# Short products of constants in TensorE's idle time, placed by the scheduler

## The chip, the cores and the metric

The kernel runs on one core of a Trainium2 chip. The metric is the device time of one execution in microseconds (us), as the median of several runs. A core has five engines that work side by side and wait for one another through semaphores: TensorE (PE) for matrix products, VectorE (DVE), ScalarE (ACT), GpSimd (POOL), and SyncE (SP), which issues the DMA transfers. PE reads its operands from SBUF and writes its results to PSUM, a memory of eight banks of 128 partitions by 512 columns of float32.

## What is computed

Two transformer blocks in a row, each with two layers, on 512 tokens of width 1024, in float32. Cut to the shape of the work:

```python
def first_block(x, ...):
    h = x
    for l in range(2):
        u = rms_norm(h, attn_norm[l])
        proj = u @ w_in[l]                       # 1024 -> 7424 columns
        a = differential_attention(...)          # 4 heads
        r = bidirectional_retention(...)         # 4 heads
        c = grouped_query_attention(...)         # 8 query heads, 2 key heads
        merged = sum(sigmoid(gate_n) * (branch_n @ w_branch[l, n]) for n, branch_n in enumerate((a, r, c)))
        h = h + merged @ w_out[l]
        m = relu(rms_norm(h, mlp_norm[l]) @ w_mlp_in[l]) ** 2
        h = h + m @ w_mlp_out[l]
    return h

def second_block(x, c, ctx, ...):                # ctx: 256 more tokens, updated in the first layer only
    for l in range(2):
        z = modulate(rms_norm(x, norm1_g[l]), ...) @ w_in[l]
        y_f, y_a, y_c = fourier_mix(...), latent_attention(...), conformer_conv(...)
        x = x + gate1 * (concat(y_f, y_a, y_c) @ w_o[l])
        x = x + gate2 * (relu(modulate(rms_norm(x, norm2_g[l]), ...) @ w_mlp1[l]) ** 2 @ w_mlp2[l])
    return rms_norm(x, final_norm_g)
```

## The kernel before

Activations lie transposed: 128 features on the partitions, tokens along the free dimension, so that 1024 features are eight tiles. Every product is done in three passes of float32r operands: a value is split into a high part (an ACT copy, `hi`) and a rest (a DVE subtraction, `lo`), and high by high, high by rest and rest by high are added up in PSUM. A weight tile of 128x1024 comes by DMA into one of three `raw` buffers, ACT writes its high part and DVE its rest into a pair of six `w` buffers (`wload`), and PE multiplies. The three passes of one step are a group: its first two products need the weight's high part, the third needs the rest that DVE writes.

The work is cut into phases: the mixer of a layer (`m10`, `m11` in the first block, `m20`, `m21` in the second) and its output projection with the MLP (`p10`, `p11`, `p20`, `p21`). Each phase has PSUM pools of its own, whose tags (`mm`, `sc`, `acc` and others) share the eight banks. Between phases the next norm is worked out in two halves of 256 tokens (`norm_split`, `factor`): squares of the features are split into a pair `x`, PE adds them over the features by a product with constants (`sums`; printed as `x,sums`), DVE takes the root in some ten short steps, and the scaled values become the operands `r` of the next phase. The last pair `x` of the second half is thus the head of a chain of PE, DVE and ACT steps that the next phase waits for.

No engine's order is written by hand. The code records its operations into a planner (`Sched`), and `run` plays a phase through on a time line of its own: each operation has a cost (`_cost`), each engine takes the ready operation of least priority number, a buffer is given when it is free on that time line. The order in which operations start there is the order in which the instructions are emitted; on the chip each engine then works through its own list in order, and waits where an operand isn't there. The time line's costs are estimates, so that an engine's idle time on it need not be idle time on the chip. A bank counts as free 0.2 us after the last step that reads it.

The constants `sums` (128x896: averages over 64, 128, 256 or 1024 features and centring matrices) come by DMA into a `raw` buffer and are copied by DVE (`V.tensor_copy(sums, ones)`, the CAST at 14.13 us in the trace).

Of the kernel before, what the change touches and what calls it, by code (L numbers as in the profile page):

```python
# [19 lines left out]
P = 128  # L20
# [36 lines left out]
HI = "A"  # L57
LO = "V"
YADD = "V"
HALVES = 'P'  # L60
SWAP8 = list(range(8, 16)) + list(range(8)) + list(range(16, 32))
SWAP16 = list(range(16, 32)) + list(range(16))
# [87 lines left out]
class Sched:  # L150


    def __init__(self, tc):
        self.tc, self.nc = tc, tc.nc
        self.tags, self.ops, self.bufs, self.bias, self.macro = {}, [], [], 0.0, None
        self.behind, self.dma, self.port = {}, 0.0, 0.0
        nc = tc.nc
        self.engines = {"PE": nc.tensor, "DVE": nc.vector, "ACT": nc.scalar, "POOL": nc.gpsimd, "SP": nc.sync}

# [111 lines left out]
    def run(self):  # L271
# [90 lines left out]
        def hold(op):  # L362
# [7 lines left out]
            coming[op.eng] = keep  # L370
            return until

        left = len(ops)
        while left:
            for e in self.engines:
                if free_at[e] > now:
                    continue
                while ready[e]:
                    op = ops[ready[e][0][1]]
                    until = None if e == "SP" else hold(op)  # L380
                    if until is not None:
                        heapq.heappush(events, (until, 0, 0))
                        break
                    heapq.heappop(ready[e])
                    if place(op):
                        order.append(op)
                        if e == "SP":
                            dma = max(dma, now + DMA) + op.cost
                            free_at[e], end = now + 0.06, dma
                        else:  # L390
                            end = free_at[e] = (max(now, port) if op.port else now) + op.cost
                            if op.port:
                                port = end
                        for n in op.nexts:
                            n.unstarted -= 1
                            n.soon = max(n.soon, end + lag(op, n))
                            if not n.unstarted:
                                coming[n.eng].append(n)
                        heapq.heappush(events, (free_at[e], 0, 0))
                        heapq.heappush(events, (end, 1, op.idx))  # L400
                        break
            if not events:
                raise RuntimeError(f"no step can go on: {left} left")
            now = events[0][0]
# [44 lines left out]
        base = free_at["PE"]  # L449
        self.behind, self.dma = {e: max(0.0, t - base) for e, t in free_at.items()}, max(0.0, dma - base)  # L450
        self.port = max(0.0, port - base)
        for b in {id(b): b for b in self.bufs}.values():
            b.at = max(0.0, b.at - base)
        for b in self.bufs:
# [68 lines left out]
def kernel(  # L523
# [42 lines left out]
    def fixed(p, cols, name, dt=F32):  # L566
        return sc.fixed(p.tile([P, cols], dt, tag=name, name=name))
# [119 lines left out]


    sums = fixed(gp, 7 * P, "sums", F32R)
    ones = sc.alloc("raw", 7 * P)  # L690
    SP.dma_start(ones, const_d[:, P:])
    V.tensor_copy(sums, ones)
# [992 lines left out]
    def phase(name, shares, slots=()):  # L1685

        with ExitStack() as st:
            p = pool(name, None, st)
            pp = pool(name + "p", bass.MemoryType.PSUM, st)
            banks.clear()  # L1690
            for tags, n in shares.items():
                tag = tags.split()[0]
                banks.update((x, tag) for x in tags.split())
                if tag == "sc2":
                    sc.slots(pp, tag, n, 1024, F32)
                    banks["sc"] = "sc2"
                else:
                    sc.slots(pp, tag, n, 512, F32)
# [267 lines left out]
```

## Time and profile before

| | us |
|---|---|
| median of 3 runs | 3541.93 |
| lowest, highest | 3540.41, 3547.73 |
| the profiled execution | 3539.29 |
| its span, first to last instruction | 3537.5 |
| PE busy in it | 3348.9 (95%) |
| DVE, ACT, POOL busy | 2285.2 (65%), 1437.3 (41%), 948.2 (27%) |
| mean granted clock of TensorE | 0.977 of full speed |

The profile is one execution, taken by the hardware's profiler. Times in it count from the span's start. A product's duration in it holds a modelled drain, so that the distance of two starts is the better measure of what a product takes in a row of products. In brackets behind a timeline row stands the idle time of the engine before it and who ended it; rows of one kind are merged, with their count behind an x. [...] All helper calls of the planner have one line number, so that groups are told apart by the tiles that they write and read (`mm<-r,w`: into a bank of tag mm, from operand r and weight w).

### The profile page before, as it was taken

Reading aid. Unit: us, or ns where it says so; the run is one execution under the profiler, and the core shown is the slowest. Engines: PE = TensorE matmul, PEld = TensorE weight load, DVE = VectorE, ACT = ScalarE, POOL = GpSimd, SP = SyncE. Lnnn points to the kernel's source line nnn. Section 1 sums busy time; section 2 is a strip of 40 time slices with the busy share of each in tenths; the row PEclk is TensorE's granted clock in tenths of the full one; section 3 lists DMA queues with packets and bytes.
Section 4 is the critical chain, followed back from the end, with each engine's and each line's share of the span. In section 5 each row is a group of like instructions: output and inputs, shape, how many; then the busy total and the mean of one; then the engine's idle time right before and its main releaser. Section 6 shows DMA issues by size and latency. Waiting matters only on the chain.

```text
span 3537.5 us, 46905 instructions
## 1 busy us (share of the span) xinstructions
PE 3348.9 (95%) x17724; PEld 2823.5 (80%) x17724; DVE 2285.2 (65%) x4048; ACT 1437.3 (41%) x2699; POOL 948.2 (27%) x886
## 2 busy tenths in 40 slices
PE   6999999999989999999999987899999988889998
PEld 6787778788877877778888776788888886878887
DVE  7787866897378878668733898552332369963334
ACT  4554443322345544443223466441221334743233
POOL 4222323211132223231101565220210235621002
PEclk9999999999999999999999999999999998999999
DMA  3121124464321112154723210211111221022222
GB/s 125 60 69 60 66 72 173 154 213 162 110 97 55 69 66 72 66 179 159 270 99 104 69 37 1 84 60 59 61 68 58 69 79 50 19 84 96 96 96 84
DMA packets 100307, 324.48 MB, mean 92 GB/s; under 512 B 11120, under 2 KB 18288, under 8 KB 100080
## 3 DMA queue, kind: packets, MB, share of 16 engines
q1 hardware_dynamic: 100080, 321.48, 26.9%
q8 instruction: 139, 2.28, 0.3%
q14 instruction: 88, 0.72, 0.1%
HBM read 312.00 MB, written 9.44 MB: 91 GB/s over the span
## 4 chain that ended last, share of the span: by engine, by line
PE 85%; DVE 9%; ACT 3%; issue 2%; POOL 1%; DMA 0%; SPq 0%; DVEq 0%; ACTq 0%; POOLq 0%
PE mm L447 79%; PE sc L447 5%; DVE r L447 2%; DVE h L447 2%; PE acc L447 2%; DVE w L447 1%; DVE s L447 1%; DVE t L447 1%; ACT r L447 1%; ACT e L447 1%; DMA raw<-in_win_dram 0%; ACT t L447 0%; ACT w L447 0%; POOL t L447 0%; POOL h L447 0%
## 5 line engine op out<-in xcount | busy, mean ns | idle before, releaser
L447 PE MATMUL mm<-r,w 128*128 128x512 f32 (+1 forms) x12134 | 2570.7, 363 | 55.1 <-DVE w L447 23.0
L447 PEld LDWEIGHTS mm<-r,w 128*128 128x128 f32 x12134 | 2041.9, 191 | 399.7 <-DVE w L447 26.2
L447 DVE TENSOR_TENSOR w<-raw,w 128x1024 fp32r<-128x1024 f32 (+1 forms) x466 | 588.0, 1268 | 736.4 <-issue 358.1
L447 ACT ACTIVATE w<-raw 128x1024 fp32r<-128x1024 f32 (+1 forms) x466 | 483.7, 1046 | 1042.1 <-PE mm L447 900.8
L447 POOL TENSOR_SCALAR e<-e,s 128x512 f32<-128x512 f32 (+1 forms) x176 | 158.1, 901 | 397.6 <-DVE s L447 377.7
L447 ACT ACTIVATE e<-sc,s 128x512 f32<-128x512 f32 (+2 forms) x208 | 153.5, 739 | 131.5 <-DVE s L447 130.0
L447 PE MATMUL mm<-rc,w 128*128 128x256 f32 x768 | 166.1, 281 | 0.0
L447 DVE TENSOR_REDUCE s<-sc 128x1 f32<-128x512 f32 (+2 forms) x208 | 152.5, 741 | 19.3 <-PE sc L447 18.9
L447 PEld LDWEIGHTS mm<-rc,w 128*128 128x128 f32 x768 | 139.8, 189 | 20.3
L447 POOL TENSOR_TENSOR t<-t,t 128x512 f32<-128x512 f32 (+2 forms) x72 | 92.4, 1285 | 189.5 <-DVE t L447 162.9
L447 PE MATMUL mm<-r,r 128*128 128x256 f32 (+1 forms) x595 | 125.5, 343 | 11.5 <-DVE r L447 6.1
L447 DVE SCALAR_TENSOR_TENSOR mraw<-mraw,mrow 128x1024 f32<-128x1024 f32 x96 | 129.8, 1362 | 4.4 <-DMA mraw<-in_wmod_dram 3.1
L447 POOL TENSOR_TENSOR x<-t,x 128x512 fp32r<-128x512 f32 (+1 forms) x58 | 82.5, 1425 | 175.1 <-ACT x L447 175.1
L447 ACT ACTIVATE r<-mm 128x256 fp32r<-128x256 f32 (+1 forms) x278 | 98.0, 401 | 63.1 <-PE mm L447 60.0
L447 DVE SCALAR_TENSOR_TENSOR h<-cu,half,h 128x512 f32<-128x512 f32 (+1 forms) x144 | 122.6, 865 | 0.8
L447 DVE TENSOR_TENSOR r<-mm,r 128x256 fp32r<-128x256 f32 (+1 forms) x264 | 105.8, 433 | 22.0 <-ACT r L447 19.9
L447 ACT ACTIVATE r<-t 128x512 fp32r<-128x512 f32 (+3 forms) x141 | 84.2, 601 | 87.9 <-DVE t L447 66.0
L447 PEld LDWEIGHTS mm<-r,r 128*128 128x128 f32 x595 | 96.9, 202 | 25.8 <-ACT r L447 6.7
L447 PE MATMUL mm<-w,r 128*128 128x256 f32 x736 | 109.7, 290 | 7.3 <-DVE w L447 5.0
L447 ACT ACTIVATE t<-mm 128x512 f32<-128x512 f32 (+4 forms) x126 | 67.7, 538 | 119.6 <-PE mm L447 117.9
L447 PEld LDWEIGHTS mm<-w,r 128*128 128x128 f32 x736 | 98.3, 195 | 11.6 <-DVE w L447 5.3
L447 DVE TENSOR_TENSOR r<-t,r 128x512 fp32r<-128x512 f32 (+2 forms) x117 | 91.8, 791 | 13.1 <-ACT r L447 10.4
(596 smaller groups left out, 4124.2 us busy)
## 6 DMA issues: line engine op xcount, KB each, us to landing
raw<-in_wm_dram SPq DMA_DIRECT2D x256, 512.0 KB, 3.5
raw<-in_win_dram SPq DMA_DIRECT2D x134, 512.0 KB, 3.5
mraw<-in_wmod_dram SPq DMA_DIRECT2D x96, 512.0 KB, 4.4
raw<-in_wbr_dram SPq DMA_DIRECT2D x24, 512.0 KB, 3.5
raw<-in_wout_dram SPq DMA_DIRECT2D x16, 512.0 KB, 4.6
raw<-in_wo_dram SPq DMA_DIRECT2D x16, 512.0 KB, 3.5
kept<-h SPq DMA_DIRECT2D x24, 256.0 KB, 3.1
h<-kept SPq DMA_DIRECT2D x24, 256.0 KB, 5.4
```

What stands on the lines that cost most here:

```text
L447: getattr(self.engines[eng], name)(*[_real(x) for x in a], **{n: _real(x) for n, x in k.items()})
```

## The change

The planner gets a list of the stretches in which PE was busy on its time line. At every event, if PE is free, it looks at the earliest time at which a next PE step can be ready (`soon`). If that is more than 0.118 us off, and PE was busy for under 55% of the last 1.7 us of the time line, and a bank of tag `mm`, `sc` or `acc` is free, it emits one product of the constants with themselves, 128x128 by 128x256, into the first free bank, and counts PE busy for 0.118 us. The bank isn't taken from the free list, and nothing reads the result: the next real user starts a new sum in it. A further event 0.118 us later is put in each time. So that the products can run before the constants are there, DVE first fills `sums` with zeros.

```diff
@@ -57,6 +57,7 @@
 YADD = "V"
+WARM = (1.7, 0.55, 0.118)
 HALVES = 'P'
@@ -154,6 +155,7 @@
         self.behind, self.dma, self.port = {}, 0.0, 0.0
+        self.warm, self.busy = None, []
         nc = tc.nc
@@ -370,6 +372,25 @@
+        busy, span, share, step = self.busy, *WARM
+
+        def warm():
+
+            if self.warm is None or free_at["PE"] > now or not left:
+                return
+            soon = min([u.soon for u in coming["PE"] if not u.unstarted], default=now + 1.0)
+            while busy and busy[0][1] <= now - span:
+                busy.pop(0)
+            done = sum(b - max(a, now - span) for a, b in busy)
+            banks = [t for n, t in self.tags.items() if n in ("mm", "sc", "acc") and t.free and t.load is not None and n in self.here]
+            if soon - now > step and done < share * span and banks:
+                op = Op()
+                op.calls = [("PE", "matmul", (banks[0].free[0][:, :256],), dict(lhsT=self.warm[:, :P], rhs=self.warm[:, :256], start=True, stop=True))]
+                order.append(op)
+                free_at["PE"] = now + step
+                busy.append((now, now + step))
+            heapq.heappush(events, (now + step, 0, 0))
+
         left = len(ops)
@@ -391,6 +412,8 @@
                             if op.port:
                                 port = end
+                            if e == "PE":
+                                busy.append((now, end))
@@ -399,6 +422,7 @@
                         break
+            warm()
             if not events:
@@ -449,6 +473,7 @@
         self.port = max(0.0, port - base)
+        self.busy = [(a - base, b - base) for a, b in busy]
@@ -687,6 +712,8 @@
     sums = fixed(gp, 7 * P, "sums", F32R)
+    V.memset(sums.bitcast(F32), 0.0)
+    sc.warm = sums.real()
     ones = sc.alloc("raw", 7 * P)
@@ -1688,6 +1715,7 @@
             banks.clear()
+            sc.here = [tags.split()[0] for tags in shares]
```

The emitted program has 771 such products, in 73 rows of 1 to 56, beside the 17,726 matrix products and transposes of before. Four of the places, with the code's names: 56 stand ahead of the first real product (53 of them ahead of the wait for the constants), 35, 32 and 55 at the ends of `p10`, `p11` and `p20`, and 43 behind the last real product. Since the products take time on the planner's time line and its events become denser, the order of the real work changes as well, by a few rows here and there from the end of `p10` on, and the numbers of the buffers with it.

PE in `m10`, where a new weight comes into use, `w_105` its high part and `w_104` its rest (the products from 57.58 us on in the trace). Before:

```order
L447 MATMUL mm_164<-r_69,w_103 128x512
L447 MATMUL mm_164<-r_68,w_102 128x512
L447 MATMUL mm_165<-w_105,r1x 128x256
L447 MATMUL mm_165<-w_104,r1x 128x256
L447 MATMUL mm_165<-w_105,r4x 128x256
L447 MATMUL mm_165<-w_105,r5x 128x256
```

After:

```order
L471 MATMUL mm_164<-r_69,w_103 128x512
L471 MATMUL mm_164<-r_68,w_102 128x512
L471 MATMUL mm_165<-sums 128x256 x23
L471 MATMUL mm_165<-w_105,r1x 128x256
L471 MATMUL mm_165<-w_104,r1x 128x256
L471 MATMUL mm_165<-w_105,r4x 128x256
L471 MATMUL mm_165<-w_105,r5x 128x256
```

23 products of the constants now stand ahead of the group's first product; the second product is the one that needs the rest `w_104`. The order of the real products is the same.

PE at the end of `p10` (about 984 to 992 us in the trace): `x,sums` are the last two sums of squares of the norm's second half, the others are products of the half that is ready (`r` the operands, `w_107` and `w_105`, `w_104` and `w_103` the two parts of two weights). Before:

```order
L447 MATMUL mm_7155<-r_62,w_105 128x256
L447 MATMUL mm_7155<-r_63,w_107 128x256
L447 MATMUL mm_7155<-r_81,w_107 128x256
L447 MATMUL mm_7155<-r_63,w_105 128x256
L447 MATMUL mm_7157<-x_114,sums 128x256
L447 MATMUL mm_7156<-r_73,w_104 128x256
L447 MATMUL mm_7156<-r_75,w_104 128x256
L447 MATMUL mm_7156<-r_73,w_103 128x256
L447 MATMUL mm_7157<-x_111,sums 128x256
L447 MATMUL mm_7156<-r_62,w_104 128x256
```

After, at the row of constants:

```order
L471 MATMUL mm_4599<-r_78,w_106 128x256
L471 MATMUL mm_4600<-sums 128x256 x35
L471 MATMUL mm_7414<-x_112,sums 128x256
L471 MATMUL mm_7414<-x_113,sums 128x256
L471 MATMUL mm_7415<-r_92,w_107 128x256
```

and some ten products further on:

```order
L471 MATMUL mm_7415<-r_70,w_107 128x256
L471 MATMUL mm_7415<-r_86,w_105 128x256
L471 MATMUL mm_7414<-x_114,sums 128x256
L471 MATMUL mm_7415<-r_82,w_107 128x256
L471 MATMUL mm_7415<-r_74,w_107 128x256
L471 MATMUL mm_7415<-r_82,w_105 128x256
L471 MATMUL mm_7414<-x_111,sums 128x256
L471 MATMUL mm_7415<-r_73,w_107 128x256
```

Before, the two last sums stand among the second group of products (`mm_7156`); now they stand among the first (`mm_7415`), some 27 products earlier, and 35 products of the constants stand ahead of all of it.

ACT at the same place: `w<-raw` casts a weight of 128x1024, `r<-h` is an operand of the second half. Before:

```order
L447 ACTIVATE x_114<-h_146 128x256
L447 ACTIVATE lge<-vec 128x8
L447 ACTIVATE w_102<-raw_109 128x1024
L447 ACTIVATE w_106<-raw_110 128x1024
L447 ACTIVATE r_92<-h_139 128x256
L447 ACTIVATE r_86<-h_145 128x256
L447 ACTIVATE r_91<-h_142 128x256
L447 ACTIVATE r_62<-h_144 128x256
```

After:

```order
L471 ACTIVATE x_114<-h_146 128x256
L471 ACTIVATE lge<-vec 128x8
L471 ACTIVATE w_102<-raw_109 128x1024
L471 ACTIVATE r_92<-h_139 128x256
L471 ACTIVATE r_86<-h_145 128x256
L471 ACTIVATE w_106<-raw_110 128x1024
L471 ACTIVATE r_91<-h_142 128x256
L471 ACTIVATE r_84<-h_140 128x256
```

The first two operands `r_92` and `r_86` now stand ahead of the cast of `raw_110` into `w_106`.

## Rows read from the trace of the kernel before

**Rows 1.** The page: busy time, share, instructions; then the chain of work.

```profile
PE 3348.9 (95%) x17724; PEld 2823.5 (80%) x17724; DVE 2285.2 (65%) x4048; ACT 1437.3 (41%) x2699; POOL 948.2 (27%) x886
...
PE 85%; DVE 9%; ACT 3%; issue 2%; POOL 1%; DMA 0%; SPq 0%; DVEq 0%; ACTq 0%; POOLq 0%
```

**Rows 2.** The view of the cores.

```profile
core 0: 3537.5 us, clock 0.977
```

**Rows 3.** Windows (from:to, length, busy us), fifteen half-clock stretches behind filled gaps.

```profile
core 0: us, PE busy (x) PEld busy (x) DVE busy (x) ACT busy (x) POOL busy (x), PEclk, DMA share, GB/s
...
985.56:988.97 3.41, 3.41 (x17) 3.25 (x16) 3.41 (x8) 2.42 (x7) 1.28 (x3) 0.50 0.25 92
...
sum 105.79, PE 72.10 PEld 61.07 DVE 97.73 ACT 23.23 POOL 22.94; mean PE 4.81 PEld 4.07 DVE 6.52 ACT 1.55 POOL 1.53
```

**Rows 4.** Windows, the other nine stretches at half clock with PE work.

```profile
sum 44.41, PE 38.22 PEld 35.74 DVE 37.55 ACT 18.74 POOL 17.44; mean PE 4.25 PEld 3.97 DVE 4.17 ACT 2.08 POOL 1.94
```

**Rows 5.** Timeline, 54-72 us: start, busy us, work, [idle ahead <- releaser].

```profile
57.58 0.28 PE L447 MATMUL mm<-w,r1x 128*128 128x256 f32 x1
...
62.68 0.58 PE L447 MATMUL mm<-w,r1x 128*128 128x256 f32 x1 [4.83 <-DVE w L447]
...
63.28 0.63 PE L447 MATMUL mm<-w,r5x 128*128 128x256 f32 x2
...
63.70 0.41 PE L447 MATMUL mm<-w,r7x 128*128 128x256 f32 x1
```

**Rows 6.** Timeline, 1943 to 1985 us.

```profile
1949.18 4.18 PE L447 MATMUL mm<-r,w 128*128 128x256 f32 x33 [1.22 <-ACT t2x L447]
...
1955.50 0.40 ACT L447 ACTIVATE x<-h 128x256 fp32r<-128x256 f32 x1
```

**Rows 7.** Timeline, 972 to 1000 us.

```profile
984.63 2.42 PE L447 MATMUL mm<-r,w 128*128 128x256 f32 x12 [1.77 <-ACT t3x L447]
...
990.23 0.40 ACT L447 ACTIVATE x<-h 128x256 fp32r<-128x256 f32 x1
...
991.86 0.28 PE L447 MATMUL mm<-x,sums 128*128 128x256 f32 x1
...
996.48 1.06 ACT L447 ACTIVATE w<-raw 128x1024 fp32r<-128x1024 f32 x1 [1.80 <-DMA raw<-in_win_dram]
...
997.44 1.32 ACT L447 ACTIVATE r<-h 128x256 fp32r<-128x256 f32 x4
...
997.89 2.32 PE L447 MATMUL mm<-r,w 128*128 128x256 f32 x8 [5.03 <-ACT r L447]
```

**Rows 8.** Windows, five of the fifteen stretches (60.55 to 3170.09).

```profile
sum 37.54, PE 21.14 PEld 20.98 DVE 36.23 ACT 6.32 POOL 2.44; mean PE 4.23 PEld 4.20 DVE 7.25 ACT 1.26 POOL 0.49
```

**Rows 9.** Windows, four of the fifteen stretches, in the second block's attention stages.

```profile
sum 27.30, PE 21.26 PEld 17.11 DVE 20.77 ACT 10.31 POOL 6.40; mean PE 5.31 PEld 4.28 DVE 5.19 ACT 2.58 POOL 1.60
```

**Rows 10.** Windows, the first of these attention stages.

```profile
2045.00:2256.00 211.00, 167.05 (x1093) 145.00 (x1091) 187.82 (x413) 144.14 (x354) 113.11 (x122) 0.94 0.10 33
```

**Rows 11.** Timeline of PE, 575 to 578 us.

```profile
577.07 1.19 PE L447 MATMUL mm<-r,w 128*128 128x512 f32 x4 [0.85 <-DVE z L447]
```

**Rows 12.** Timeline of all engines, 0 to 30 us.

```profile
14.13 0.62 DVE L447 CAST sums<-raw 128x896 fp32r<-128x896 f32 x1
...
20.19 1.36 PE L447 MATMUL mm<-x,sums 128*128 128x256 f32 x3 [4.10 <-ACT x L447]
```

**Rows 13.** Timeline, 3524 to 3538 us.

```profile
3527.18 0.39 PE L447 MATMUL ms<-x,sums 128*128 128x256 f32 x1 [0.32 <-DVE x L447]
```

**Rows 14.** Timeline, 2862 to 2912 us.

```profile
2880.09 0.58 PE L447 MATMUL mm<-x,sums 128*128 128x256 f32 x1 [2.10 <-ACT x L447]
...
2889.78 0.40 ACT L447 ACTIVATE x<-h 128x256 fp32r<-128x256 f32 x1
...
2896.92 0.52 PE L447 MATMUL mm<-r,w 128*128 128x256 f32 x1 [3.90 <-ACT r L447]
```

## Prediction, written before the changed kernel ran

> **What bounds the kernel now.** I read the page first: the shares of the engines and the chain of work that ended last [rows 1]. TensorE (PE) is busy 95% of 3537.5 us and holds 85% of that chain, so a microsecond of PE work that goes away is in most places a microsecond of time. Its mean granted clock is 0.977 [rows 2]. Then I read stretches of busy time. [...] From 57.58 to 62.68 us PE waits for a weight from VectorE (DVE); behind that gap products of 256 columns stand 0.21 us apart (two from 63.28 to 63.70) [rows 5]. At full clock 33 of them take 4.18 us from 1949.18 on, the last one's 0.28 us among it [rows 6]: 3.90/32 = 0.12 us apart. At full clock such work takes 0.12/0.213 = 56% of its time at half clock: 44% of it can be won and no more.
>
> **What the change can win.** It puts 771 products of 128x256 constants into 73 places of PE's order, each worth 0.12 us at full clock. Fifteen of the 24 stretches get such products in the gap just ahead of them; PE was busy for 72.1 us in these [rows 3]. At full clock that work takes 44% less: 72.1 x 0.44 = 31.7 us, the most that the filling can give. (The view's busy time holds the modelled drain of each product, so the figure is high rather than low.) The other nine stretches, 38.2 us of PE work [rows 4], get no products in their gap or are changed by the moved order, which comes further down.
>
> How much of the 31.7 comes? The planner paces its products to 55% of its own time line, but on the chip nothing paces them. The row of 23 at 57.58 runs through back to back, 23 x 0.12 = 2.8 us at the front of a gap of 5.0, and leaves 2.2 us idle behind it [rows 5]. The product at 984.63 stands 2.05 us behind the one before it (1.77 us idle by the view) [rows 7], and the clock is at 0.50 from 985.56 on [rows 3]. So what is left is about as long as what lost the clock once. Five stretches (60.55, 627.16, 1026.52, 2330.41, 3170.09) keep such a rest, 1.9 to 2.6 us by the same working; their PE work was 21.1 us [rows 8], worth 9.3, and I take half of it as lost: 4.6 us. Four (2238.25, 2248.49, 2972.12, 3074.52), with 21.3 us [rows 9], worth 9.4, lie in the two attention stages of the second block. In the first of these DVE is busy 188 of 211 us and PE only 167 [rows 10], so a faster PE mostly waits sooner; I let a quarter stand, 7.0 us lost. **31.7 - 4.6 - 7.0 = 20.1 us won.**
>
> **What the products cost.** Where the real gap is as long as the planner's they cost nothing: DVE's weight, or ScalarE's (ACT's) operand, is late anyway and hides them. The row of 23 pushes back one product of 0.28 us, whose follower waits for DVE until 62.68 in any case [rows 5]; the like holds for the rows of 12 to 37 ahead of a group whose third product waits for a weight. If that weight came 2.8 us sooner, the row would stand on the path in full. The cover fails where the gap is shorter than the row. At 577.07, 16 products (1.9 us) meet 0.85 us of idle [rows 11]: +1.0 us, and the same once more in the second layer, +1.0. At the start three products stand behind the CAST that makes the constants at 14.13, ahead of the first sums of squares: 0.36 to 0.64 us on the first norm's path; the 22 behind these meet 4.1 us of idle [rows 12] and need 2.6 us at full clock, 4.7 at half. I take +1. The 53 ahead of the CAST are over in time: even 0.21 us apart they take 11 us. Single rows of 2 to 5 products at places without a gap: +2 in all, bounds 0 and 4. Sum **+5.0**. The 43 products at the end stand behind PE's last real one at 3527.18 [rows 13]; they end 5 to 9 us later, inside the 10 us that the tail still takes, so they cost nothing.
>
> Seven real products now wait for PE's own earlier ones, all at a change of stage. No row shows such a wait. Its bounds are nothing, where the operand comes later anyway, and the 0.28 us of one product's modelled duration [rows 5]; I take 0.2 each, nearer to the second since PE has to come to rest: **+1.4**. The rows' first products also wait for the last reader of the bank they write. In nearly all places the next real product takes the same bank and had that wait before, so nothing is added.
>
> **What moves.** At three borders of stages the row is longer than the gap and the order of real work changes too. (a) At 984.63: 35 products, 4.2 us, in a gap of 2.05. But the last two sums of squares of the norm's second half (x, sums) come some 27 products earlier in PE's order. They can run once ACT has written x at 990.23 + 0.40 and DVE its rest; in the trace PE comes to the last of them only at 991.86. PE will now stand before them from about 988.6 to 990.7, and the norm's chain begins 0.7 us earlier. On ACT the first operand r is moved ahead of a weight's cast that ended only at 997.54 and so held r back to 997.44 [rows 7]. PE's wait up to 997.89 should end near 996: -2. (b) At 1949.18: 32 products, 3.8 us, in 1.22 us of idle; x is ready at 1955.90, PE waits for it some 3 us, and the chain gains under 1 us [rows 6]: +2, with the clock perhaps lost. (c) At 2880.09: 55 products, 6.6 us, against 2.1 us of idle; the last x (ACT, 2889.78) is taken about 2 us earlier than in the trace, so the wait that ended at 2896.92 [rows 14] moves up, but PE stands some 4 us before that x and loses the clock. Ends: -3.5 if the whole chain moves, +1 if only the row's excess is left; I take -2, since the wait at 2896.92 is one for that chain. Sum **-2.0**, bounds -6 and +5. In the attention stages of the second block some hundred further steps change places by a few rows; no row prices that: 0, bounds -5 and +5.
>
> **Sum.** -20.1 + 5.0 + 1.4 - 2.0 = -15.7 us. The profiled execution took 3539.3 us, 1.8 more than its span and 2.6 less than the median of the three runs, 3541.9. Taken from the median: **3526 us**.
>
> **The rivals.**
> (1) Every gap that is filled keeps the clock, and PE's time is worth as much everywhere: 31.7 instead of 20.1 us, -27.3, 3514 us. For it: what is left of the gaps is nowhere longer than 2.6 us. Against it: the 2.05 us at 984.63. [...] Chance 0.14.
> (2) The clock stays up, but waits take the time back: behind most gaps the next wait is DVE's or ACT's, and an earlier PE waits earlier. If a third of the 31.7 us stands: -10.6 + 5.0 + 1.4 - 2.0 = -6.2, 3536 us. For it: DVE's 188 of 211 us [rows 10]. Against it: PE's 85% of the chain [rows 1]. Chance 0.18.
> (3) **Slower:** products of constants don't hold the clock, so nothing of the 20.1 us is won. The costs stay, +5.0 + 1.4, and the borders stand at +3 instead of -2, since their rows take up to 0.21 us a product: +9.4, 3551 us. The long rows decide: if the clock behind 62.68 still stands at 0.50 in spite of the row of 23, this is the case. For it: no row shows a product whose result goes nowhere, and the first 53 multiply zeros. Against it: every stretch of real products in the trace brought the clock up, sums against the same constants among them. [...] Chance 0.15.
>
> **How the numbers follow.** Forecast 0.53, rivals 0.14, 0.18 and 0.15. Some 0.2% (7 us) is what a measurement of this kernel can tell from no change. Faster: nearly all of the forecast's share and rival 1's, 0.65; same: rival 2 and the forecast's weak end, 0.19; slower: rival 3 and a bad turn of the moved order, 0.16. The range reaches from rival 1 with its borders at their best, 3511, to 3543, which takes in rival 2 and the bounds of the order and leaves out rival 3.
>
> **What will show it.** The mean granted clock should rise from 0.977 to 0.985 or more, and the stretches at 367.75 and 1333.72, whose gaps the rows fill, should stand at 1.00 with products 0.12 us apart. The first weight's products at 22 us should start no earlier, since the start is ACT's and DVE's. The waits that ended at 997.89 and 2896.92 should end earlier, and the product at 577.07 should start 1 us later against its neighbours. The forecast is wrong if the clock's mean stays under 0.98, if the attention stages (2045 to 2256, 2983 to 3120) change by over 5 us, or if the borders (b) and (c) lose more than 3 us each.

## The result and the profile after

| | before | after |
|---|---|---|
| median of 5 runs, us | 3546.55 | 3527.59 |
| profiled execution, us | 3539.29 | 3520.30 |
| its span, us | 3537.5 | 3518.4 |
| mean granted clock | 0.977 | 0.993 |

The ratio of after to before is 0.9944 (95% interval 0.9928 to 0.9960): 0.56% or some 20 us faster. Forecast were 3526 us, 15.7 us below a median of 3541.9. The two later runs of before stood at 3547, so that the drop is nearer 20 than 16. One of the five executions of after took 4184.14 us at a mean clock of 0.75; it is in the median and left out of the ratio.

The page of after, parts 1, 4 and 5, and the view of the cores; they answer to [rows 1] and [rows 2]. Part 5 gives busy time and mean ns of one, then the idle time ahead.

```profile
PE 3407.0 (97%) x18495; PEld 2893.4 (82%) x18495; DVE 2302.4 (65%) x4049; ACT 1435.6 (41%) x2699; POOL 947.8 (27%) x886
...
PE 85%; DVE 9%; ACT 3%; issue 1%; POOL 1%; DMA 0%; SPq 0%; DVEq 0%; ACTq 0%; POOLq 0%
...
L471 PE MATMUL mm<-sums 128*128 128x256 f32 x759 | 106.8, 290 | 5.5 <-DVE sums L471 5.5
```

```profile
core 0: 3518.4 us, clock 0.993
```

The products add 771 instructions and 108 us of busy time (12 more stand in banks of tag `sc`), and PE is busier by only 58 us. The 50 us between the two are not all won, since the modelled drain of such a product lies over real products too: counted alone in the trace, the real products keep PE busy for 3316.4 us, 32.5 less than the 3348.9 of before. The chain's shares are nearly those of before; the gain is in the speed of PE's part, not in who ends last.

The windows of the half-clock stretches of after answer to [rows 3] and [rows 4]. Columns: from:to, length, busy us (instructions) of PE, PEld, DVE, ACT, POOL, the granted clock as a share of full speed (the traces of before and after hold 0.50 and 1.00 and no other level, half and full clock below; a window over both shows the mean), the DMA share, GB/s.

```profile
12.47:19.30 6.83, 5.53 (x26) 5.53 (x27) 5.43 (x18) 5.04 (x14) 4.57 (x6) 0.50 0.92 314
63.67:67.09 3.42, 3.42 (x16) 3.02 (x15) 2.89 (x4) 0.99 (x2) 0.00 (x0) 0.50 0.81 211
2026.34:2033.16 6.82, 5.54 (x18) 4.77 (x19) 5.84 (x16) 0.63 (x1) 4.30 (x5) 0.50 0.14 58
...
sum 48.20, PE 42.97 PEld 40.02 DVE 41.19 ACT 18.03 POOL 29.17; mean PE 3.58 PEld 3.33 DVE 3.43 ACT 1.50 POOL 2.43
```

Without the first row (in the trace of before the clock is recorded only from 26 us on) 37.4 us of PE work ran at half clock, against 110.3 before, in the 15 and 9 stretches of [rows 3] and [rows 4]. The difference of 72.9 us, times 44%, is 32 us that the clock gave (44% by the distances in the trace of before: products of 256 columns start 0.213 us apart from 63.28 to 65.20 us, at a clock of 0.50, and 0.12 at 1.00), which agrees with the 32.5 us of the real products. The time fell by 19 to 20. So some 12 us went elsewhere, and the experiments had to say where.

One gap shows what a filled one looks like. The timeline of PE at the second weight that comes late, first before, then after (start, busy us, work, idle ahead):

```profile
368.61 0.63 PE L447 MATMUL mm<-r1x,w 128*128 128x512 f32 x1
...
371.59 0.79 PE L447 MATMUL mm<-r1x,w 128*128 128x512 f32 x1 [1.93 <-DVE w L447]
372.18 0.63 PE L447 MATMUL mm<-r5x,w 128*128 128x512 f32 x1
372.61 0.63 PE L447 MATMUL mm<-r7x,w 128*128 128x512 f32 x1
```

```profile
367.94 1.84 PE L471 MATMUL mm<-sums 128*128 128x256 f32 x14
369.62 0.40 PE L471 MATMUL mm<-r1x,w 128*128 128x512 f32 x1
...
371.19 0.50 PE L471 MATMUL mm<-r1x,w 128*128 128x512 f32 x1 [0.94 <-DVE w L471]
371.52 0.39 PE L471 MATMUL mm<-r5x,w 128*128 128x512 f32 x1
371.75 0.40 PE L471 MATMUL mm<-r7x,w 128*128 128x512 f32 x1
```

The weight's rest ends the wait in both. Before, products of 512 columns then follow 0.43 us apart, at a clock of 0.50; after, 0.23 us apart, at 1.00. The row of 14 takes 1.68 us in front of a wait that is there anyway, so it costs nothing.

### The profile page after: what moved, and what is told of

It reads as the page before. It is cut to its first block, busy times and chain, and to the rows that moved or that the text cites. A ratio compares the mean times of both kernels' runs of the same rounds, so it can differ in the third digit from the quotient of the medians.

```text
span 3518.4 us, 48429 instructions
## 1 busy us (share of the span) xinstructions
PE 3407.0 (97%) x18495; PEld 2893.4 (82%) x18495; DVE 2302.4 (65%) x4049; ACT 1435.6 (41%) x2699; POOL 947.8 (27%) x886
## 4 chain that ended last, share of the span: by engine, by line
PE 85%; DVE 9%; ACT 3%; issue 1%; POOL 1%; DMA 0%; SPq 0%; DVEq 0%; ACTq 0%; POOLq 0%
PE mm L471 78%; PE sc L471 5%; DVE r L471 2%; DVE h L471 2%; PE acc L471 2%; DVE w L471 1%; DVE t L471 1%; DVE s L471 1%; ACT r L471 1%; ACT e L471 1%; DMA raw<-in_win_dram 0%; ACT t L471 0%; ACT w L471 0%; POOL t L471 0%; DVE x L471 0%
## 5 line engine op out<-in xcount | busy, mean ns | idle before, releaser
L471 DVE TENSOR_TENSOR w<-raw,w 128x1024 fp32r<-128x1024 f32 (+2 forms) x466 | 592.5, 1277 | 728.3 <-issue 356.8
L471 ACT ACTIVATE r<-t 128x512 fp32r<-128x512 f32 (+2 forms) x143 | 85.0, 598 | 81.8 <-DVE t L471 64.0
L471 PE MATMUL mm<-sums 128*128 128x256 f32 x759 | 106.8, 290 | 5.5 <-DVE sums L471 5.5
L471 PEld LDWEIGHTS mm<-sums 128*128 128x128 f32 x759 | 100.6, 198 | 7.1 <-DVE sums L471 5.7
```

What stands on the lines that cost most here:

```text
L471: getattr(self.engines[eng], name)(*[_real(x) for x in a], **{n: _real(x) for n, x in k.items()})
```

## Where the time went, place by place

Since no real product was added, the n-th real product of one trace can be set beside the n-th of another. The table gives the time between two such products, less the same in the first profile of before; between the places every trace agrees with before to 0.2 us. Places are named by us of before.

```
place (us of before)        before  order  products  after  p11  cap8  drop16  no_att.
                             again   only      only         old
15-56    start                 0.0    0.5      -0.4    0.4  0.2   0.3     0.9     0.4
56-361   first weight         -0.2    0.2      -0.6   -0.5 -0.6   0.6    -0.5    -0.6
361-407                        2.9   -1.4      -2.9   -2.9 -2.8  -2.9    -2.9    -2.9
575-580  row of 16             0.0    0.0       1.1    1.1  1.1   0.2     0.0     1.1
620-642                        0.1    0.7      -1.3   -1.3 -1.3   0.1    -1.3    -1.3
982-1011 border (a)            0.4    0.5       0.4   -2.0  0.8  -2.0     0.6    -2.3
1011-1045 row of 23           -0.2    0.2      -0.1   -1.6 -0.3   0.9    -0.2    -1.6
1327-1371                      0.0    2.5      -1.6   -1.7 -1.7  -1.7    -1.7    -1.7
1538-1544 row of 16            0.0    0.0       1.1    1.1  1.1   0.2     0.0     1.1
1584-1607                      0.0   -1.5      -2.3   -3.2 -3.2  -3.2    -3.2    -3.2
1947-2001 border (b)           0.0    3.5       2.1    1.5  2.1   2.9     2.8     2.7
2001-2015 a norm behind it     0.0   -4.6      -1.3   -4.6 -1.3  -4.6    -4.6    -4.6
2015-2048 attention's head     0.0    4.4       1.0    5.1  0.9   5.5     4.8     4.0
2048-2200 first attention      0.3    5.4       3.7    2.1  2.6   5.3     4.7     5.4
2200-2268 its end              1.3    0.7      -3.6   -3.5 -3.1  -3.1    -3.7     0.1
2325-2349                     -0.7    0.1      -2.3   -2.3 -0.8  -0.1    -2.3    -2.3
2876-2931 border (c)          -0.6   -4.7      -1.8   -3.8 -4.9  -4.8    -3.5    -3.5
2931-2995 behind it           -0.3    1.4      -1.5    0.2  1.3   1.3     0.4     0.4
2995-3165 second attention    -0.4    0.0      -0.3   -1.1  0.0   1.5     1.4     1.1
3165-3184                      0.2    0.0      -0.4   -1.7 -1.7   0.8    -1.7    -1.7
whole span                     3.0    7.8     -10.7  -19.1-12.1  -3.6   -10.5    -8.4
```

A single profile is worth less than its decimals: at 361 us the same kernel needed 2.9 us more in its second profile. Verdicts on whole kernels below go by the timed runs, and the table only says where to look.

The same pairing says where the 12 us went. Between two such products, the time in which PE is busy with real products can be counted apart from the rest (idle, or products of constants alone). In after against before the first is 32.5 us less and the second 13.5 us more. Of these, 4.8 us stand at 2931 to 2995, 2.6 at the start, 2.2 at the two rows of 16, 1.8 at border (b) and 1.0 at border (a). At the largest of these places the real products took 4.6 us less and the time didn't fall; PE there, first before, then after:

```profile
2940.49 8.67 PE L447 MATMUL mm<-r,w 128*128 128x512 f32 x28 [3.30 <-DVE w L447]
...
2976.35 1.65 PE L447 MATMUL mm<-r,w 128*128 128x512 f32 x3 [2.57 <-DVE t L447]
```

```profile
2925.70 6.68 PE L471 MATMUL mm<-r,w 128*128 128x512 f32 x28 [0.84 <-DVE w L471]
...
2942.34 0.50 PE L471 MATMUL mm<-x,sums 128*128 128x512 f32 x1 [1.29 <-POOL x L471]
...
2961.33 1.45 PE L471 MATMUL mm<-r,w 128*128 128x512 f32 x3 [3.25 <-DVE t L471]
```

With the rows in the gap the clock is 1.00 from 2915 to 2961 us of after (before, 0.50 from 2934.57 to 2944.81), and the 28 products take 6.7 us instead of 8.7. Then PE waits for POOL, which it did not before, and longer for DVE's t. From 2876 to 2995 every changed version in the table ends 3.0 to 3.6 us ahead of before, order_only (3.3), which puts nothing into this gap, among them, so what the rows gave there did not decide when the last wait ended.

## Experiments

Eight of the edits below use one helper that leaves out or lengthens single rows of products without touching the planner's order; rows are counted from 0.

```diff
+    def rows(self, order):
+        for op in order:
+            if op.eng == "WARM":
+                self.row += not self.count
+                self.count += 1
+                if self.count <= ROWS.get(self.row, 1000):
+                    yield op
+                last = op
+            else:
+                if op.eng == "PE" and self.count:
+                    for _ in range(self.count, ROWS.get(self.row, 0)):
+                        yield last
+                    self.count = 0
+                yield op
...
+                op.eng = "WARM"
...
-        for op in order:
+        for op in self.rows(order):
```

### The order alone, and the products alone

The changed kernel does two things, and the prediction's terms hang on which of them works. In order_only the helper gives no product at all (`if self.count <= 0`).

> The planner plans with the products as in the changed kernel, but none is emitted: the new order of the real work alone. Theory (the products hold the clock; the new order is worth a few us at the border at 984 and in the norms behind 1949 and 2880): 2 to 8 us faster than before, mean granted clock still 0.974 to 0.980, gaps at 366, 625, 1332 and 1586 as before with half clock behind them. Rival (the new order carries the gain and the products are only passengers): 15 to 20 us faster, like the changed kernel.

Measured: 1.0006 of before (0.9997 to 1.0015), clock 0.974. **The new order alone gives nothing.** It is not neutral inside: the table shows 4.6 us won at 2001 to 2015, 3.3 from border (c) to 2995, and 9.8 us lost from 2015 to 2200.

In products_only the planner looks between two events of its own, and takes no time for the products:

```diff
-                free_at["PE"] = now + step
-                busy.append((now, now + step))
-            heapq.heappush(events, (now + step, 0, 0))
+            at = max(now, filled[0])
+            while banks and at < min(events[0][0], soon - step):
...
+                    order.append(op)
+                    busy.append((at, at + step))
+                at += step
+                filled[0] = at
```

> The order of before, word for word, with 818 products put into the same kinds of gaps by the same rule, without time on the planner's time line. Theory: 11 to 17 us faster than before, clock 0.988 to 0.993; up to the end of the first block's first layer place by place as in the changed kernel (3.5 us gained by 640 us), and then 3 to 6 us less than it, because at 984, 1949 and 2880 the rows are longer than the gaps and nothing moves ahead to make up for it. Rival (the order carries the gain): within 4 us of before, or slower. Rival (waits give the clock's gain back): 3 to 8 us faster with the clock at 0.99.

Measured: 0.9943 (0.9930 to 0.9955), clock 0.991. Up to 640 us the table is that of after to 0.1 us but for the start. **The products carry the whole gain**, and the rival in which the order carries it falls. That they would give less than the changed kernel was wrong: the ratios are the same.

### Does the clock ask what PE multiplies?

The third rival of the prediction was that such products don't count. Two runs change what PE does in the gaps: zeros, and transposes.

```diff
+    zeros = fixed(gp, 2 * P, "zeros", F32R)
-    V.memset(sums.bitcast(F32), 0.0)
-    sc.warm = sums.real()
+    V.memset(zeros.bitcast(F32), 0.0)
+    sc.warm = zeros.real()
```

> The changed kernel with the products taken from a tile of zeros that is never loaded with the constants. Theory (a product holds the clock whatever it multiplies): as the changed kernel, 16 to 22 us faster than before, clock 0.989 to 0.993. Rival (data that don't change anything don't count): 0 to 12 us slower than before, clock 0.972 to 0.980, half clock behind the gaps at 366 and 1332 us again.

Measured: 0.9937 (0.9924 to 0.9949), clock 0.992. Zeros serve as well as constants.

```diff
-op.calls = [("PE", "matmul", (banks[0].free[0][:, :256],), dict(lhsT=self.warm[:, :P], rhs=self.warm[:, :256], start=True, stop=True))]
+op.calls = [("PE", "transpose", (banks[0].free[0][:, :P], self.warm[:, :P].bitcast(F32), self.ident), {})]
...
+ROWS = {0: 0, 1: 0, 2: 0, 3: 0, 4: 0, 5: 0, 6: 0}
...
+    sc.ident = ident.real()
```

> The changed kernel with each product from the 20th microsecond on behind the first weights replaced by a 128x128 transpose of constants on TensorE (they follow each other in 0.11 us in the trace of before, the products in 0.12); the seven rows of the first 35 us are left out. Theory by the rows (the clock asks only whether TensorE works): as the changed kernel, 15 to 21 us faster than before, clock 0.987 to 0.993. Rival (transposes don't count as work): the rows' costs stay and the clock is lost as before, 2 to 10 us slower than before, clock 0.972 to 0.980.

Measured: 0.9944 (0.9932 to 0.9957), clock 0.989. The timeline of this kernel, at the place shown above:

```profile
366.82 1.69 PE L489 MATMUL mm<-ident,sums 128*128 128x128 f32 x14
368.27 0.48 PE L489 MATMUL mm<-r1x,w 128*128 128x512 f32 x1
368.59 0.39 PE L489 MATMUL mm<-r4x,w 128*128 128x512 f32 x1
370.06 0.50 PE L489 MATMUL mm<-r1x,w 128*128 128x512 f32 x1 [1.08 <-DVE w L489]
370.39 0.39 PE L489 MATMUL mm<-r5x,w 128*128 128x512 f32 x1
370.62 0.40 PE L489 MATMUL mm<-r7x,w 128*128 128x512 f32 x1
```

Behind 14 transposes, 0.10 us each, the products follow 0.23 us apart, as they do at a clock of 1.00 in after. So transposes in float32 between real products hold the clock here; whether transposes alone would bring it up, no run here shows.

### How long must a row be?

Every row is cut to 8 products (`if self.count <= ROWS.get(self.row, 8)`).

> The changed kernel with every row cut to its first 8 products: 397 instead of 771; the order of the real work is the same. Theory (what is left idle of a gap decides whether the clock falls): the rows of 9 to 55 now leave 0.1 to 5.7 us more idle, so half clock comes back at about half of the fifteen places, and the excess of the long rows goes too: 8 to 14 us faster than before, clock 0.981 to 0.988. Rival (a few products in a gap are enough to hold the clock): 20 to 24 us faster than before, clock 0.989 to 0.993.

Measured: 0.9962 (0.9949 to 0.9974), 13 us, clock 0.984: as the theory said. The short gaps kept their gain with 8 products (361, 1327 and 1584 us); at 56, 620, 1011, 2325 and 3165, where a row had been cut by up to 17 products, it was gone.

In long_rows three rows are made as long as their gaps (`ROWS = {7: 42, 45: 31, 62: 21}`).

> The changed kernel with three rows made as long as their gaps: 42 products instead of 23 at the first weight (57.6 us), 31 instead of 17 and 21 instead of 8 in the second block's attention stages (2250 and 3073 us in the trace of before), 46 products more in all. Theory of the prediction (the rest of a gap that a row leaves, 1.7 to 2.2 us, can still lose the clock): the half clock at 63.7 us (3.4 us long) goes away and 1 to 2 us are gained there, no more than 1 us at each of the others; 1 to 3 us faster than the changed kernel. Rival (rests of that length are harmless, the half clock there has another cause): no change, or 0.5 us slower at each place where the row ends behind the wait.

Measured: 0.9934 (0.9922 to 0.9947), clock 0.993; against the changed kernel's 0.9944 no difference that the intervals show. By its trace the first gap is filled to the end, and 2.0 us instead of 0.5 are won there:

```profile
57.67 5.19 PE L489 MATMUL mm<-sums 128*128 128x256 f32 x42
62.70 0.51 PE L489 MATMUL mm<-w,r1x 128*128 128x256 f32 x2
```

Whether a row of 23 is enough there is a matter of the execution. Here are the windows behind that row, first of the changed kernel, then of no_five, which has the same row at that place:

```profile
60.42:63.67 3.25, 1.14 (x10) 0.94 (x9) 3.25 (x6) 0.28 (x1) 0.00 (x0) 1.00 0.00 0
63.67:67.08 3.41, 3.41 (x16) 3.02 (x15) 2.89 (x4) 0.99 (x2) 0.00 (x0) 0.50 0.81 210
```

```profile
60.22:63.47 3.25, 1.13 (x10) 0.93 (x9) 3.25 (x6) 0.28 (x1) 0.00 (x0) 1.00 0.00 0
63.47:66.88 3.41, 3.41 (x20) 2.40 (x19) 3.32 (x5) 0.98 (x2) 0.00 (x0) 1.00 0.66 197
```

The same 23 products and the same idle time behind them (2.11 and 2.12 us by the timelines): the one lost the clock, the other kept it. Of eight profiles with 22 or 23 products (or transposes) there, one kept it; both with 42 did (long_rows and best). At 1011 us, with a like row and 2.29 us left, two of ten kept it. At 620, 2325 and 3165, with 1.71, 2.28 and 1.64 us left in the trace of after, it was nine, eight and nine of ten. So a rest of that size is a chance, and its length alone doesn't set the odds: what tells 2325 from 1011 stays open.

### The rows that are longer than their gaps

> The changed kernel's order, five rows of products left out: 16 ahead of the products that stood at 577 and 1540 us in the trace of before, and the 35, 32 and 55 at the ends of p10, p11 and p20. Theory (a row that is longer than its gap pushes the products behind it back by the excess, and only that): 1.1 us faster than the changed kernel at each of the two rows of 16; at the row of 32, 3 to 5 us earlier right behind it, of which little is left 15 us later, where ACT and DVE end the wait; at 35 and 55 half clock returns for 3 to 7 us, and no change or up to 1.5 us slower by the end of the next wait. Together 2 to 4 us faster than the changed kernel. Rival (these rows hold the clock for what follows): 3 to 6 us slower than the changed kernel.

Its edit is `ROWS = {15: 0, 19: 0, 29: 0, 35: 0, 52: 0}`. Measured: 0.9940 (0.9927 to 0.9954), no different from the changed kernel, and neither theory's figure for the whole. By place, each row of 16 gives its 1.1 us back. At (a) and (b) the profile reads 2.4 and 1.4 us later than after, but profiles that have these rows read the same (drop16: 0.6 and -1.8), so the rows of 35 and 32 are not shown to matter. At (c) the row of 55 did nothing (-3.6 up to 2995 with it and without it).

> The changed kernel without the two rows of 16 products in a gap of 0.85 us (577 and 1540 us in the trace of before). Theory (a row longer than its gap costs its excess and holds nothing there): 2.2 us faster than the changed kernel by the trace (1.1 at each place), so a ratio to before of 0.9935 to 0.9942 and no half clock behind either place. Rival (the rows hold the clock there): half clock for 3 to 7 us behind each, 1 to 4 us slower than the changed kernel.

Its edit is `ROWS = {15: 0, 29: 0}`. Measured: 0.9935 (0.9922 to 0.9949). The whole can't be told from the changed kernel, the place can. After, then drop16:

```profile
572.69 2.07 PE L471 MATMUL mm<-sums 128*128 128x256 f32 x16
574.82 2.56 PE L471 MATMUL mm<-r,w 128*128 128x512 f32 x10
```

```profile
573.96 4.38 PE L489 MATMUL mm<-r,w 128*128 128x512 f32 x18 [0.85 <-DVE z L489]
```

Drop16 has the 0.85 us of [rows 11] again. With the row, the products behind it come 1.1 us later against their neighbours, at both places and in all seven profiles that have the full rows (1.0 with transposes); without it, 0.0, and the 18 products behind follow 0.23 us apart, as at full clock. With 8 products (cap8) it is 0.2: a row that about fits its gap is nearly free.

### The second block's first attention stage

Here the changed kernel gave back 7.2 us (2015 to 2200), which no term of the prediction had; nor had it the 4.6 us won just ahead, at 2001 to 2015. Was the first profile of before only a lucky one?

> The kernel before, profiled once more. Open: the changed order (order_only) is 8.7 us later than the first profile of before between the products at 2015 and 2200 us in the second block's first attention stage, while it is no slower as a whole. Theory (one execution of a kernel differs from the next in which gaps lose the clock, and the first profile of before was a short one): this profile needs 3 to 9 us more than the first one's 185.4 us for that stretch, and the span is 3540 to 3547 us. Rival (the moved order costs 4 to 9 us there): 184 to 187 us again.

Measured: 3542.3 us, one execution. The stretch took 0.3 us more than in the first profile. The theory falls as far as two profiles can tell: before's time there is steady. The timelines of PE where the stage begins, of the changed kernel, of order_only, and of p11_old (below), which has the order of before there:

```profile
2015.07 8.00 PE L471 MATMUL mm<-r,w 128*128 128x512 f32 x44
2027.62 10.72 PE L471 MATMUL mm<-r,w 128*128 128x256 f32 x46 [4.55 <-DVE t L471]
```

```profile
2042.24 10.85 PE L489 MATMUL mm<-r,w 128*128 128x256 f32 x46 [4.58 <-DVE t L489]
```

```profile
2033.21 8.24 PE L482 MATMUL mm<-r,w 128*128 128x256 f32 x46 [0.48 <-DVE r L482]
```

The wait of 4.6 us is there without a single product, and it is gone with the old order. What PE waits for is a transposition on DVE, which itself stands behind POOL:

```profile
2020.68 3.38 POOL L471 TENSOR_TENSOR t<-t,t 128x512 f32<-128x512 f32 x2 [6.05 <-DVE t L471]
2024.16 1.27 POOL L471 TENSOR_SCALAR t<-cu,half 128x512 f32<-128x512 f32 x1
2025.51 2.92 POOL L471 TENSOR_TENSOR h<-h,t 128x512 f32<-128x512 f32 x2
```

```profile
2027.12 0.45 DVE L471 STREAM_TRANSPOSE t<-mm 128x256 f32<-128x256 f32 x1 [1.15 <-POOL h L471]
```

Behind this wait the clock is at 0.50 (the window from 2026.34 above), so the 46 products take 10.7 us instead of 8.2. The planner put no product into this gap; whether its time line has none there, or no bank was free, is not shown. Which of the moved rows makes the wait was not tried.

The wait stands against others that the new order takes away. PE behind border (b), first before, then after:

```profile
1961.97 0.38 PE L447 MATMUL mm<-r,w 128*128 128x256 f32 x1 [0.57 <-ACT r L447]
1963.56 6.13 PE L447 MATMUL mm<-r,w 128*128 128x256 f32 x49 [1.21 <-DVE r L447]
1971.00 31.00 PE L447 MATMUL mm<-r,w 128*128 128x256 f32 x198 [1.31 <-DVE w L447]
2003.12 0.49 PE L447 MATMUL mm<-x,sums 128*128 128x512 f32 x1 [1.12 <-ACT x L447]
2004.24 0.38 PE L447 MATMUL mm<-x,sums 128*128 128x256 f32 x1 [0.63 <-ACT x L447]
2005.16 0.50 PE L447 MATMUL mm<-x,sums 128*128 128x512 f32 x1 [0.54 <-POOL x L447]
```

```profile
1945.08 0.39 PE L471 MATMUL mm<-x,sums 128*128 128x256 f32 x1 [2.14 <-ACT x L471]
...
1945.94 48.76 PE L471 MATMUL mm<-r,w 128*128 128x256 f32 x341
1994.53 0.40 PE L471 MATMUL mm<-x,sums 128*128 128x512 f32 x1
```

Before, PE waits three times for a norm's x from 2003 us on, and the clock is at 0.50 from 2006.14 to 2009.56; in after that norm's products find their x ready. This is the -4.6 of the table, there without any product too, and against it stands +5.1 (after) or +4.4 (order_only) at the attention's head.

p11_old keeps the order of before in this stage, by letting the products take no time in phase `p11`:

```diff
+OLD = ("p11",)
...
+            old = self.name in OLD
+            at = max(now, filled[0]) if old else now
+            until = min(events[0][0], soon - step) if old else soon - step
...
+                    if not old:
+                        free_at["PE"] = now + step
```

> The changed kernel, but in the phase p11 the products take no time on the planner's time line, so that p11 and the attention stage behind it keep the order of before; the borders of p10 and p20 keep the new order. 787 products. Theory (the moved order of p11 and of the attention stage is worth nothing on balance): within 3 us of the changed kernel, 16 to 22 us faster than before. Rival (the moved order costs 4 to 9 us in the attention stage): 23 to 29 us faster than before.

Measured: 0.9939 (0.9927 to 0.9951): within 3 us of the changed kernel, as the theory had it. The old order saves 4.2 us at the stage's head and gives up 4.0 between 1947 and 2015, 3.3 of it at that norm. The new order moves a wait, it does not shorten the way.

From 2048 to 2200 the loss isn't shown to be the order's. After is 2.1 us later there than before; products_only and p11_old, both with the order of before in that stretch, are 3.7 and 2.6 us later, and order_only, without products, 5.4. In all four the real products' busy time grew, by 2.2, 4.4, 2.7 and 5.9 us, and the rest of the time did not grow; in after the clock is at 0.50 in four windows of 3.41 us there, in before in three. Why these products take longer there than in the two profiles of before, under either order, stays open.

In no_attention the rows of both attention stages are left out (`ROWS = {i: 0 for i in [*range(36, 48), *range(58, 66)]}`, and 0 products for these).

> The changed kernel without its twenty rows of products in the two attention stages of the second block (133 products of 771); the order of the real work is the same. The prediction let a quarter of 9.4 us stand for these rows: 1 to 4 us slower than the changed kernel, 16 to 19 us faster than before. Rival (PE's time is worth as much there as elsewhere): 6 to 10 us slower than the changed kernel, 10 to 13 us faster than before. Rival (they are worth nothing, because VectorE ends the next wait): as the changed kernel, within 1 us.

Measured: 0.9959 (0.9946 to 0.9973), clock 0.988: 0.0015 or 5 us above the changed kernel, with intervals that overlap, and between the figures of the prediction and of the first rival. The windows from the 9,760th to the 10,850th real product (2048 to 2259 us in before), first of the changed kernel, then of no_attention:

```profile
2039.49:2248.66 209.17, 173.19 (x1155) 151.47 (x1153) 187.44 (x404) 142.98 (x352) 115.21 (x128) 0.96 0.10 33
```

```profile
2040.61:2256.81 216.20, 173.58 (x1093) 150.46 (x1092) 188.20 (x405) 143.53 (x354) 115.42 (x128) 0.91 0.11 38
```

DVE is the busiest engine in both. Yet the stretch is 7.0 us shorter in this pair where PE's clock stands at 0.96 rather than 0.91: DVE's share doesn't make PE's time worthless.

### All together

best leaves out the two rows of 16 and lengthens three rows (`ROWS = {7: 42, 15: 0, 29: 0, 45: 31, 62: 21}`).

> The changed kernel without the two rows of 16 (577 and 1540 us) and with the three lengthened rows (42, 31 and 21 products), 785 products in all. If both edits keep what they gave alone: 2 to 4 us faster than the changed kernel, a ratio to before of 0.9925 to 0.9940. Rival (executions differ by more than either edit is worth): no difference from the changed kernel that five rounds can show.

Measured: 0.9944 (0.9931 to 0.9956), clock 0.992. The places are as wanted (0.0 at both rows of 16, 2.0 us won at the first weight), and the whole is the changed kernel's. Edits of 1 to 2 us drown in what executions differ by. No version tried beats the changed kernel by more than the intervals.

## Why the prediction was right, and where only by cancelling

- **The filled gaps.** Forecast -20.1, and -2 at border (a), which the table can't part from them. Measured in after, at 56, 361, 620, 982, 1011, 1327, 1584, 2200, 2325, 2995 and 3165: -21.8. The working held: PE work at half clock (72.1 us) times 44%, less a part for rests and for attention. Half for the five stretches with a rest was right as a mean over executions (29 of 48 kept the clock), but it isn't one half at each: two places mostly lost it, three mostly kept it. A quarter for attention was too little: 5 us of 9.4 by no_attention. Two of the fifteen stretches, at 2934 and 2972, stand behind border (c); there the time didn't fall although the real products took 4.6 us less.
- **The rows' costs.** The two rows of 16: +1.0 each forecast, +1.1 measured, by the sum as worked out (16 products against 0.85 us). The start: +1 forecast, +0.4. For single short rows +2 and for PE's own waits +1.4 were put in; between the places no trace differs by more than 0.2 us, so these 3.4 us are not seen. Of the second, what falls at the borders was not taken apart. That PE has to come to rest there, the reason for taking 0.2 us each, no run shows. The 43 products at the end cost nothing that shows.
- **Border (a).** -2 forecast and -2.0 measured, but not by the reason given. The order alone gives +0.5, and of the eight profiles with the changed kernel's order and the row of 35, three show -2.0 to -2.3, one -0.9 and four +0.6 to +0.8. In drop16, one of the four, 45 products from 994 us on take 7.5 us, in after 47 take 6.2, at a clock of 1.00: what is won is the speed of a later stretch, and not in every profile.
- **Border (b).** +2 forecast, +1.5 measured up to 2001 us, and by the steps as worked out: PE stood before x for 2.14 us, and the row's excess came back in part, since the waits for r and w behind it went away. In drop16, no_attention, transposes and best it is 2.7 to 2.9.
- **Border (c).** -2 forecast, -3.6 measured up to 2995. That the moved sums did it is not shown: the order alone gives -3.3 and the products in the order of before -3.3 too, so that the two don't add up.
- **The moved steps in attention.** 0 with bounds of 5 either way. Measured were -4.6 at 2001 to 2015, +5.1 to 2048 and +2.1 to 2200, together +2.6. The sum lies inside the bounds, but by luck: this step had no row to price it, its first two parts are each about as large as a bound, both lie ahead of the attention, where the prediction had not looked, and the third isn't shown to be the order's.
- **The rivals.** The third falls: the clock stays up with rows of constants (mean 0.993), of zeros (0.992) and of transposes (0.989), against 0.977 before. The first is bounded by the row of 23: 0.50 came back at 63.67. The second has some truth: beside 32.5 us less of real products' time there are 13.5 more of other time. But that isn't so behind most gaps: at 361, 620, 1011, 1327, 1584, 2325 and 3165 the time fell by what the real products gave, to 0.4 us; it is a few places, 2931 to 2995 above all.

The clock came out at 0.993, where 0.985 or more was forecast; the first weight's products didn't start earlier (22.05 against 22.10 us); the stretches at 367 and 1333 stand at 1.00. The products there are 0.23 us apart: the 0.12 us of the prediction is the distance at 256 columns, and these have 512.

By place, in the order gaps with border (a), rows of 16, start, border (b), border (c), moved steps, short rows and own waits: forecast -22.1 + 2.0 + 1.0 + 2.0 - 2.0 + 0 + 3.4 = -15.7, measured -21.8 + 2.2 + 0.4 + 1.5 - 3.6 + 2.6 + 0 = -18.7 in the one profile of after. The largest terms were right by their working. The moved steps cost 2.6 us that were not forecast, and border (c) and the short rows and waits, with 1.6 and 3.4 us, more than made up for them.

## What to carry to other kernels

In a kernel like this one, with PE at 85% of the chain and 110.3 us of its work at a clock of 0.50 behind gaps, work that nobody reads can hold the clock, and which of three kinds it was made no difference that the intervals show (ratios 0.9944 with products of constants, 0.9937 with zeros, 0.9944 with transposes). The row should end near the end of the gap: here rows that left some 1.6 to 2.3 us lost the clock in 19 of 48 cases, and 16 products in a gap of 0.85 us cost 1.1 us. Find out first whether such a change also moves the order of the real work, and run the order alone and the filling alone: here the order was worth nothing as a whole and 3 to 5 us either way at single places. Sum by places, and compare the places too, since a right total can be made of wrong steps.

## What the runs showed that was not expected

The same row, with the same 2.1 us left idle behind it, kept the clock in one execution and lost it in the next; at 361 us two profiles of the very same kernel differ by 2.9 us. Transposes in float32 held the clock as well as products did (0.989 against 0.993, ratios both 0.9944). And although PE holds 85% of the chain, 32 us of its clock were worth only some 20 us of time: from 2931 to 2995 us none of the 4.6 us that the real products gave was left when DVE ended the last wait.
